# Block sums of the MLP's down weights formed in HBM by copies and accumulating transfers, ahead of the stages that use them

## The chip, the cores and the metric

The kernel runs on one core of one Trainium2 chip. The metric is the device time of one execution in microseconds (us). Shown for the kernel before are three timed runs and one profiled execution.

## The reference

A two-layer decoder trunk on 528 tokens (16 learned meta tokens and 512 inputs), model width 1024: layer 0 is a forgetting attention, layer 1 a gated linear recurrence (HGRN2), and each is followed by a gated MLP with a hidden width of 2816. The change concerns the last product of that MLP:

```python
def conv_ffn(h, norm_g, w_gate, w_up, conv_w, conv_b, w_down):
    xn = rms_norm(h, norm_g)
    a = xn @ w_gate
    ...
    return (jax.nn.silu(a) * (xn @ w_up)) @ w_down
```

`w_down` has 2816 x 1024 values in float32, once for each layer.

## The kernel before

Activations stand transposed: 128 features on the partitions, tokens along the free dimension. A matrix product is done in float32r, with each operand split in a high part and a low rest (`hi` and `lo`, a cast on ScalarE and a subtraction on VectorE), and three matmuls for a block: hi by hi, hi by rest, rest by hi. The stages stand one behind the other: attention (`fox`), MLP of layer 0 (`ffn`), recurrence (`hgrn`), MLP of layer 1 (`ffn` again). In the MLP the stretch of hidden features is worked off in two runs: a run of six (twelve blocks of 128 hidden features, in two halves of r = 6) and a run of five (ten blocks, r = 5).

In each run there are two parts:

- **The hidden part.** `hidden` makes one block of hidden features: two weight tiles `gu` (gate and up, 512 KB each, loaded by `weights`, line 191), 48 matmuls with each in layer 0 (24 of 512 columns with the up tile in layer 1), a causal convolution on VectorE (lines 1056 and 1057) and the gating. In layer 0 the two leading columns of the tile `A` are set to zero by GpSimd (line 1046), and the convolution reads them. `forms` then makes seven combinations of the token halves, as Strassen's scheme in Winograd's form needs them (the two index directions are the halves of the hidden features and the halves of the tokens).
- **The down part.** For each of four pairs of output blocks, `down` does seven products of r x 3 matmuls (126 in a run of six, 105 in a run of five), where four weight blocks w11, w12, w21, w22 (128 x 768 or 128 x 640 values) enter alone or as sums: s1 = w21 + w22, s2 = s1 + w11, s3 = s2 - w22 (that is w21 + w11), s4 = s2 + w12. Here the kernel before loads the four blocks and forms the four sums on VectorE at lines 1113, 1145, 1153 (by the helper at line 124) and 1156. All seven weight blocks are then split (`parts`: the cast at line 1097, the subtraction by line 124).

Buffers: `raw` has two (the `gu` weights, and w21 and w22 of a pair: w21's becomes s1 and then s2), `hi` and `lo` three each, `temp` eight of 768 columns (the tiles A, t, s, ta, tb of the hidden part, and w11, w12, s3, s4 of the down part). The four PSUM tiles of a pair are named psp (two), psc and psd.

What sets the order: each engine works off its instructions in the order that a scheduler has given them, which weighs the program by a simulated timeline. SP (SyncE) issues every transfer, in its own order, and an issue that waits holds back those behind it. GpSimd has only some memsets and, at the start, seven additions.

In the run of five of layer 0, VectorE and ScalarE also do the work for the next stage within the down part: squares and their sum (lines 268 and 269), and the split of finished rows of `h` (lines 275 and 276).

Of the kernel before, what the change touches and what calls it, by code (L numbers as in the profile page):

```python
# [12 lines left out]
F32 = mybir.dt.float32  # L13
# [4 lines left out]
ALU = mybir.AluOpType  # L18
# [3 lines left out]
P = 128  # L22
D = 1024
KT = D // P
# [2 lines left out]
HF = 16  # L27
NPAIR = 8
NEARLY = 4
FF = 2816  # L30
NF = FF // P
EPS = 1e-6
# [42 lines left out]
def halves(t0):  # L75

    n = (T - t0) // 4 * 2
    return [(t0, n), (t0 + n, T - t0 - n)]


class Builder:
# [44 lines left out]
    def setup(self):  # L126
        nc = self.nc
        cp = self.cp = self.pool("const")
        self.h = cp.tile([P, KT, T], F32, name="h")
        self.vec = cp.tile([P, V_END], F32, name="vec")  # L130
        nc.sync.dma_start(self.vec, self.a["vec"])
        self.wraw = self.pool("wraw", 2)
        self.whi = self.pool("whi", 3)
        self.wlo = self.pool("wlo", 3)
        q, k = (self.weights(self.a["wqk"][0, i], KT, parts=2) for i in range(2))
        order = [(q, 0), 0, (k, 0), 1, 2, 3, (q, 1), (k, 1), 4, 5, 6, 7]
        for x in order:
            if isinstance(x, int):
                nc.sync.dma_start(self.h[:, x, :], self.a["h0"][:, x, :])
            else:  # L140
                x[0][3][x[1]]()
        self.first = q[:3], k[:3]
        cst = cp.tile([P, C_END], F32, name="cst")
        self.cst = cst
        nc.sync.dma_start(cst, self.a["cst"])
        self.ident = cst[:, C_ID : C_ID + P]
        self.identr = cp.tile([P, P], F32R, name="identr")
        nc.vector.tensor_copy(self.identr, self.ident)
        self.xhi = cp.tile([P, KT, T], F32R, name="xhi")
        self.xlo = cp.tile([P, KT, T], F32R, name="xlo")  # L150
        self.x = [(self.xhi[:, k, :], self.xlo[:, k, :]) for k in range(KT)]
        self.rsb = cp.tile([P, T], F32, name="rsb")
        self.onesd = cp.tile([P, 2], F32, name="onesd")
        nc.vector.memset(self.onesd, 1.0 / D)
        self.tiny = self.pool("tiny", 2)
        self.sqp = self.pool("sqp", 2)
        self.ps = self.pool("ps", 1, PSUM)
        self.nbank = 0
        self.ss = None
# [16 lines left out]
    def weights(self, src, n, w=P, parts=1):  # L176

        nc = self.nc
        raw = self.wraw.tile([P, 8 * P], F32, name="raw", tag="raw")[:, : n * w]
        hi = self.whi.tile([P, 8 * P], F32R, name="hi", tag="hi")[:, : n * w]  # L180
        lo = self.wlo.tile([P, 8 * P], F32R, name="lo", tag="lo")[:, : n * w]

        def load(c):
            nc.sync.dma_start(raw[:, c], src[:, c])
            nc.scalar.copy(hi[:, c], raw[:, c])
            self.sub(lo[:, c], raw[:, c], hi[:, c].bitcast(F32))

        self.raw = raw
        u = hi.rearrange("p (k c) -> p k c", c=w), lo.rearrange("p (k c) -> p k c", c=w), n
        if parts == 1:  # L190
            nc.sync.dma_start(raw, src)
            nc.scalar.copy(hi, raw)  # L192
            self.sub(lo, raw, hi.bitcast(F32))
            return u
        m = n * w // parts
        return *u, [partial(load, slice(i * m, i * m + m)) for i in range(parts)]

    def proj_unit(self, ps, units, x, t0, tn, prev=None):

# [124 lines left out]
    def fox(self, ctx):  # L324
# [274 lines left out]
        def stage_p():  # L599

            for m in range(NEARLY):
                nc.sync.dma_start(self.h[:, m, :], a["h0"][:, m, :])
# [159 lines left out]
    def hgrn(self, ctx):  # L762
        nc, tc, a = self.nc, self.tc, self.a
        mm = nc.tensor.matmul
        full = [(0, 264), (264, 264)]
        late = halves(A1)
        sp = self.pool("hg1", 1, ctx=ctx)
        s2 = self.pool("hg2", 2, ctx=ctx)
        ohi = sp.tile([P, KT, T], F32R, name="ohi")
# [251 lines left out]
    def ffn(self, ctx, layer, a0, o0):  # L1021

        nc, a = self.nc, self.a
        ga, up = (halves(t0) if T - t0 > 512 else [(t0, T - t0)] for t0 in (a0, o0))
        gcol, cw, cb = ((V_FFN0, V_CW0, V_CB0), (V_FFN1, V_CW1, V_CB1))[layer]
        sp = self.pool(f"ffn1_{layer}", 1, ctx=ctx)
        s2 = self.pool(f"ffn2_{layer}", 2, ctx=ctx)
# [37 lines left out]
        def temp(w, name):  # L1065
            return s2.tile([P, 6 * P], F32, name=name, tag="temp", bufs=8)[:, :w]
# [25 lines left out]
        def parts(raw):  # L1092

            w = raw.shape[1]
            hi = self.whi.tile([P, 8 * P], F32R, name="hi", tag="hi")[:, :w]
            lo = self.wlo.tile([P, 8 * P], F32R, name="lo", tag="lo")[:, :w]
            nc.scalar.copy(hi, raw)  # L1097
            self.sub(lo, raw, hi.bitcast(F32))
            return hi, lo

        def block(mp, c0, r, m, half, raw):
            k0 = (c0 + half * r) * P
            nc.sync.dma_start(raw, a[f"dn{layer}"][2 * mp + m][:, k0 : k0 + r * P])
            return raw

        def ready(mp, c0, r):

            x, w22 = (self.wraw.tile([P, 8 * P], F32, name="raw", tag="raw")[:, : r * P] for _ in range(2))
            w11 = block(mp, c0, r, 0, 0, temp(r * P, "w11"))
            p11 = parts(w11)  # L1110
            block(mp, c0, r, 1, 0, x)
            block(mp, c0, r, 1, 1, w22)
            nc.vector.tensor_tensor(x, x, w22, ALU.add)
            return w11, x, w22, p11, parts(x)

        def down(mp, c0, r, fhi, flo, last, first):

            def product(ps, w, f, start):
                hi, lo = w
                mm = nc.tensor.matmul
                for k in range(r):
                    c = slice(k * P, k * P + P)
                    xh, xl = fhi[:, f, k, :], flo[:, f, k, :]
                    mm(ps, hi[:, c], xh, start=start and k == 0, stop=False, skip_group_check=not start)  # L1127
                    mm(ps, hi[:, c], xl, start=False, stop=False, skip_group_check=not start)  # L1128
                    mm(ps, lo[:, c], xh, start=False, stop=k == r - 1, skip_group_check=not start)  # L1129

            def put(m, half, ps, op, store=False):
                c = o0 + half * hw
                hv = self.h[:, 2 * mp + m, c : c + hw]
                nc.vector.tensor_tensor(hv, hv, ps, op)
                if store and last and layer == 1:
                    nc.sync.dma_start(a["out"][2 * mp + m][:, half * hw : half * hw + hw], hv)

            A, D = (self.bank("p")[:, :hw] for _ in range(2))
            B, C = (self.bank(x)[:, :hw] for x in "cd")
            w11, x, w22, p11, ps1 = first or ready(mp, c0, r)  # L1140
            product(A, p11, 0, True)
            nc.scalar.copy(B, A)
            product(D, ps1, 3, True)
            put(1, 1, D, ALU.subtract)
            nc.vector.tensor_tensor(x, x, w11, ALU.add)
            product(B, parts(x), 4, False)
            nc.scalar.copy(C, B)
            put(0, 1, B, ALU.add)
            w12 = block(mp, c0, r, 0, 1, temp(r * P, "w12"))
            product(A, parts(w12), 1, False)  # L1150
            put(0, 0, A, ALU.add, True)
            s3, s4 = temp(r * P, "s3"), temp(r * P, "s4")
            self.sub(s3, x, w22)
            product(C, parts(s3), 5, False)
            put(1, 1, C, ALU.subtract, True)
            nc.vector.tensor_tensor(s4, x, w12, ALU.add)
            product(D, parts(s4), 2, False)
            put(0, 1, D, ALU.add, True)
            product(C, parts(w22), 6, False)
            put(1, 0, C, ALU.subtract, True)  # L1160
            if last and layer == 0:
                self.sumsq(2 * mp)
                self.sumsq(2 * mp + 1)


        for x in "cd":
            nc.tensor.matmul(self.bank(x)[:, :hw], self.xhi[:, 0, :P], self.xhi[:, 0, :hw], start=True, stop=True)
        for c0, r in ((0, 6), (12, 5)):
            fhi, flo = (sp.tile([P, 7, 6, hw], F32R, name=nm, tag=nm)[:, :, :r, :] for nm in ("fhi", "flo"))
            first = []  # L1170
            for j in range(r):
                early = None if j < r - 1 else lambda: first.append(ready(0, c0, r))
                forms(j, c0, r, fhi, flo, early)
            for mp in range(KT // 2):
                down(mp, c0, r, fhi, flo, c0 > 0, first.pop() if first else None)
# [99 lines left out]
```

## Time and profile before

| What | Value |
|---|---|
| Median of three runs | 1494.14 us (1490.6 to 1495.14) |
| Profiled execution, its own time | 1491.77 us |
| Its span, first to last instruction | 1489.7 us |
| Mean granted TensorE clock | 0.994 |
| VectorE, ScalarE and GpSimd busy | 68%, 42%, 2% of the span |
| Transfers of the SP queue | 131.58 MB, 28.4% of the 16 DMA engines' span |
| Transfers issued by GpSimd | none |

The page gives busy time by engine, and groups of instructions by line of the kernel. The view of windows gives the busy time of each engine in a stretch, with the number of instructions that touch it, the granted clock (PEclk) and the share of DMA engines that were busy. PE is TensorE, PEld its weight loads, DVE VectorE, ACT ScalarE, POOL GpSimd, SP SyncE. The chain of waits is followed back from the last instruction, so it names only what the end hung on.

### The profile page before, as it was taken

The page shows a single profiled execution, that of the slowest core. Times are in us where ns is not written, and L with a number is a line of the kernel's source. Part 1 is how long each engine was busy: PE and PEld are TensorE (multiplying, and loading weights), DVE is VectorE, ACT ScalarE, POOL GpSimd, SP SyncE. Part 2 cuts the span into 40 slices and gives each one's busy share as a digit, 9 for nine tenths or more (in the row PEclk, how much of TensorE's full clock was granted, in tenths as well). Part 3 has the DMA queues.
Part 4 walks back from the last instruction along what each step waited for, and adds up shares of the span by engine and source line. Part 5 has one row for each costly group of instructions (what it writes and reads, how often), then busy time and mean ns, then how long its engine had stood idle before and what let it go on. Part 6 is the DMA issues. An engine that isn't in the chain of part 4 may idle for free.

```text
span 1489.7 us, 28745 instructions
## 1 busy us (share of the span) xinstructions
PE 1457.1 (98%) x11620; PEld 1361.3 (91%) x11620; DVE 1010.8 (68%) x2147; ACT 627.2 (42%) x1214; POOL 33.5 (2%) x113
## 2 busy tenths in 40 slices
PE   7999999999999999999989999999999999999998
PEld 6888888988999999999889999999999999999988
DVE  7555555776576787666876667677567667767676
ACT  5355555654343343333543333333343344343433
POOL 6000000000000000000000000000000000000000
PEclk9999999999999999999999999999999999999999
DMA  4433344412323222222221201211132223332232
GB/s 157 117 103 88 102 96 121 133 52 81 113 86 100 89 86 96 100 100 79 89 78 59 85 29 58 72 58 58 57 100 86 95 90 89 96 114 89 91 103 87
DMA packets 48283, 133.39 MB, mean 90 GB/s; under 512 B 7816, under 2 KB 10376, under 8 KB 48152
## 3 DMA queue, kind: packets, MB, share of 16 engines
q1 hardware_dynamic: 48152, 131.58, 28.4%
q8 instruction: 91, 1.49, 0.4%
q14 instruction: 40, 0.33, 0.1%
HBM read 116.10 MB, written 2.10 MB: 79 GB/s over the span
## 4 chain that ended last, share of the span: by engine, by line
PE 86%; DVE 7%; DMA 4%; ACT 2%; issue 1%; SPq 1%; ACTq 0%; DVEq 0%
PE psp L206 12%; PE psp L209 12%; PE psp L210 12%; PE pss L210 8%; PE pss L206 8%; PE pss L209 8%; PE psp L255 5%; DVE lo L124 2%; DMA raw<-dn 2%; PE psc L739 2%; PE pss L890 1%; PE psp L1127 1%; PE psp L1128 1%; PE psp L1129 1%; ACT hi L1097 1%
## 5 line engine op out<-in xcount | busy, mean ns | idle before, releaser
L206 PE MATMUL psp<-xhi,hi 128*128 128x264 f32 (+3 forms) x1160 | 353.2, 305 | 6.2 <-ACT xhi L275 6.2
L209 PE MATMUL psp<-xlo,hi 128*128 128x264 f32 (+3 forms) x1160 | 354.0, 305 | 3.5 <-DVE xlo L276 3.5
L210 PE MATMUL psp<-xhi,lo 128*128 128x264 f32 (+3 forms) x1160 | 353.1, 304 | 0.0
L192 ACT CAST hi<-raw 128x1024 fp32r<-128x1024 f32 (+1 forms) x170 | 174.8, 1030 | 345.5 <-PE psp L209 118.4
L124 DVE TENSOR_TENSOR lo<-raw,hi 128x1024 fp32r<-128x1024 f32 (+3 forms) x222 | 251.1, 1132 | 77.8 <-ACT hi L192 65.1
L206 PEld LDWEIGHTS psp<-xhi,hi 128*128 128x128 f32 x1160 | 219.7, 190 | 17.8 <-ACT xhi L275 6.2
L210 PE MATMUL pss<-xhi,lo 128*128 128x264 f32 (+2 forms) x824 | 233.7, 284 | 0.0
L209 PEld LDWEIGHTS psp<-xlo,hi 128*128 128x128 f32 x1160 | 220.0, 190 | 14.7 <-DVE xlo L276 4.2
L206 PE MATMUL pss<-xhi,hi 128*128 128x264 f32 (+2 forms) x824 | 233.1, 283 | 0.0
L209 PE MATMUL pss<-xlo,hi 128*128 128x264 f32 (+2 forms) x824 | 233.0, 283 | 0.0
L210 PEld LDWEIGHTS psp<-xhi,lo 128*128 128x128 f32 x1160 | 220.1, 190 | 8.8 <-issue 1.0
L206 PEld LDWEIGHTS pss<-xhi,hi 128*128 128x128 f32 x824 | 155.3, 189 | 0.9
L209 PEld LDWEIGHTS pss<-xlo,hi 128*128 128x128 f32 x824 | 155.1, 188 | 0.9
L210 PEld LDWEIGHTS pss<-xhi,lo 128*128 128x128 f32 x824 | 154.9, 188 | 0.0
L1127 PE MATMUL psp<-fhi,hi 128*128 128x264 f32 (+1 forms) x352 | 101.0, 287 | 2.8 <-ACT hi L1097 2.1
L1129 PE MATMUL psp<-fhi,lo 128*128 128x264 f32 (+1 forms) x352 | 100.5, 286 | 1.1 <-DVE lo L124 1.0
L1128 PE MATMUL psp<-flo,hi 128*128 128x264 f32 (+1 forms) x352 | 99.6, 283 | 0.0
L1127 PEld LDWEIGHTS psp<-fhi,hi 128*128 128x128 f32 x352 | 66.5, 189 | 4.8 <-ACT hi L1097 4.6
L255 PE MATMUL psp<-hi,xhi 128*128 128x256 f32 x232 | 67.4, 290 | 2.3 <-ACT v L542 2.3
L1129 PEld LDWEIGHTS psp<-fhi,lo 128*128 128x128 f32 x352 | 66.6, 189 | 2.5 <-DVE lo L124 2.5
L255 PE MATMUL psp<-lo,xhi 128*128 128x256 f32 x232 | 66.6, 287 | 0.2 <-DVE lo L124 0.2
L1128 PEld LDWEIGHTS psp<-flo,hi 128*128 128x128 f32 x352 | 66.5, 189 | 0.1
(434 smaller groups left out, 2966.0 us busy)
## 6 DMA issues: line engine op xcount, KB each, us to landing
raw<-gu SPq DMA_DIRECT2D x88, 512.0 KB
pk<-stg SPq DMA_DIRECT2D x48, 264.0 KB
raw<-wqk SPq DMA_DIRECT2D x14, 512.0 KB
raw<-dn SPq DMA_DIRECT2D x16, 384.0 KB
w<-dn SPq DMA_DIRECT2D x16, 384.0 KB
raw<-dn SPq DMA_DIRECT2D x16, 320.0 KB
w<-dn SPq DMA_DIRECT2D x16, 320.0 KB
raw<-wv SPq DMA_DIRECT2D x8, 512.0 KB
```

Of the source, the lines that this page charges most:

```text
L124: self.nc.vector.tensor_tensor(out, x, y, ALU.subtract)
L192: nc.scalar.copy(hi, raw)
L206: ins = mm(ps, hi[:, i, :], xh, start=k == 0, stop=False)
L209: mm(ps, hi[:, i, :], xl, start=False, stop=False)
L210: mm(ps, lo[:, i, :], xh, start=False, stop=k == total - 1)
L255: mm(ps[:tn, :256], y[:, t0 : t0 + tn], w, start=n == 0, stop=n == 23)
L739: ins = mm(o, v[:kn, j, 2 * (p % 2) + hd, :], w[hd][0], start=j == 0, stop=j == last)
L890: mm(pl[:, 64 * c : 64 * c + 64], kp[:, t0 : t0 + tn], q, start=True, stop=True)
L1097: nc.scalar.copy(hi, raw)
L1127: mm(ps, hi[:, c], xh, start=start and k == 0, stop=False, skip_group_check=not start)
L1128: mm(ps, hi[:, c], xl, start=False, stop=False, skip_group_check=not start)
L1129: mm(ps, lo[:, c], xh, start=False, stop=k == r - 1, skip_group_check=not start)
```

## The change

The four sums are no longer formed on VectorE. `sum_blocks` gives each its own tile in HBM: SP copies one block there (HBM to HBM), and GpSimd issues accumulating transfers that add the others (`out += y`, done by the DMA engines). For each pair and run that makes four copies and five accumulations (s2 takes two, and s4's reads the finished s2), over both layers 64 copies and 80 accumulations. One sum is put in after each weight load that `weights` does: those of layer 0 begin with the first `gu` tile of its MLP, those of layer 1 with the first weights of the recurrence. In the down part all seven blocks of a pair are loaded, three from `dn` and four from the sums, each into a buffer of `temp`, and are split as before. `block` and `ready` go, and the two `raw` buffers stay with the other weights.

```diff
+RUNS = [(0, 6), (12, 5)]
...
+        self.hbm = self.pool("hbm", 1, bass.MemoryType.DRAM)
+        self.sums = {}
+        self.summing = iter(())
...
         if parts == 1:
-            nc.sync.dma_start(raw, src)
+            self.load = nc.sync.dma_start(raw, src)
+            next(self.summing, None)
             nc.scalar.copy(hi, raw)
             self.sub(lo, raw, hi.bitcast(F32))
             return u
...
+    def sum_blocks(self, layer):
+
+        nc = self.nc
+        for mp, c0, r in [(mp, *run) for run in RUNS for mp in range(KT // 2)]:
+            src = lambda m, half: self.a[f"dn{layer}"][2 * mp + m][:, (c0 + half * r) * P : (c0 + half * r + r) * P]
+            s1, s2, s3, s4 = self.sums[layer, mp, c0] = [
+                self.hbm.tile([P, r * P], F32, name=f"s{i}", tag=f"s{i}_{layer}_{mp}_{c0}") for i in range(1, 5)
+            ]
+            w11, w12, w21, w22 = src(0, 0), src(0, 1), src(1, 0), src(1, 1)
+            for out, x, *rest in (s1, w21, w22), (s2, w21, w22, w11), (s3, w11, w21), (s4, w12, s2):
+                self.after(nc.sync.dma_start(out, x), self.load)
+                for y in rest:
+                    nc.gpsimd.dma_start(out, y, accum_op=ALU.add, max_dma_last_dim=4 * r * P)
+                yield 1
...
+        self.summing = self.sum_blocks(1)
...
+        if layer == 0:
+            self.summing = self.sum_blocks(0)
...
-        def ready(mp, c0, r):
-
-            x, w22 = (self.wraw.tile([P, 8 * P], F32, name="raw", tag="raw")[:, : r * P] for _ in range(2))
-            w11 = block(mp, c0, r, 0, 0, temp(r * P, "w11"))
-            p11 = parts(w11)
-            block(mp, c0, r, 1, 0, x)
-            block(mp, c0, r, 1, 1, w22)
-            nc.vector.tensor_tensor(x, x, w22, ALU.add)
-            return w11, x, w22, p11, parts(x)
+        def left(mp, c0, r, i):
+
+
+            raw = temp(r * P, "left")
+            if isinstance(i, int):
+                src = self.sums[layer, mp, c0][i - 1]
+            else:
+                k0 = (c0 + i[1] * r) * P
+                src = a[f"dn{layer}"][2 * mp + i[0]][:, k0 : k0 + r * P]
+            nc.sync.dma_start(raw, src)
+            return parts(raw)
...
-            w11, x, w22, p11, ps1 = first or ready(mp, c0, r)
-            product(A, p11, 0, True)
+            ws = lambda i: left(mp, c0, r, i)
+            product(A, first[0] if first else ws((0, 0)), 0, True)
             nc.scalar.copy(B, A)
-            product(D, ps1, 3, True)
+            product(D, first[1] if first else ws(1), 3, True)
             put(1, 1, D, ALU.subtract)
-            nc.vector.tensor_tensor(x, x, w11, ALU.add)
-            product(B, parts(x), 4, False)
+            product(B, ws(2), 4, False)
             nc.scalar.copy(C, B)
             put(0, 1, B, ALU.add)
-            w12 = block(mp, c0, r, 0, 1, temp(r * P, "w12"))
-            product(A, parts(w12), 1, False)
+            product(A, ws((0, 1)), 1, False)
             put(0, 0, A, ALU.add, True)
-            s3, s4 = temp(r * P, "s3"), temp(r * P, "s4")
-            self.sub(s3, x, w22)
-            product(C, parts(s3), 5, False)
+            product(C, ws(3), 5, False)
             put(1, 1, C, ALU.subtract, True)
-            nc.vector.tensor_tensor(s4, x, w12, ALU.add)
-            product(D, parts(s4), 2, False)
+            product(D, ws(4), 2, False)
             put(0, 1, D, ALU.add, True)
-            product(C, parts(w22), 6, False)
+            product(C, ws((1, 1)), 6, False)
             put(1, 0, C, ALU.subtract, True)
...
-                early = None if j < r - 1 else lambda: first.append(ready(0, c0, r))
+                early = None if j < r - 1 else lambda: first.append([left(0, c0, r, i) for i in ((0, 0), 1)])
```

The first place is GpSimd's queue, from the last memsets of the attention to the first of the recurrence, in the kernel before. `negm` and `ssum` belong to the attention, `rowsel`, `qp` and `qk` to the recurrence.

```order
L662 MEMSET ssum 128x6
L661 MEMSET negm 128x6
L1046 MEMSET A 128x2 x22
L774 MEMSET rowsel 128x512
L840 MEMSET qp 128x14
L844 MEMSET qk 128x21
```

In the changed kernel the same queue has accumulating transfers between those memsets. The piece is from the hidden part of the first run of layer 0: the `A` tiles are those of its third, fourth, fifth and sixth block of hidden features; s1 to s4 are the tiles in HBM.

```order
L1069 MEMSET A_5476 128x2
L215 DMA s1_5763<-dn0 128x768
L215 DMA s2_5764<-dn0 128x768
L1069 MEMSET A_5617 128x2
L215 DMA s2_5764<-dn0 128x768
L215 DMA s3_5765<-dn0 128x768
L1069 MEMSET A_5755 128x2
L215 DMA s4_5766<-s2_5764 128x768
L215 DMA s1_6042<-dn0 128x768
L1069 MEMSET A_5896 128x2
```

Each memset now stands behind two or three transfers; the second one into s2_5764 has to wait for the first, and that into s4_5766 for the second.

The second place is SP's queue at the end of the hidden part of that run, before: the last `gu` tile and the loads of the first two pairs.

```order
L191 DMA raw_6667<-gu0 128x1024
L1103 DMA raw_6673<-dn0 128x768
L1103 DMA raw_6674<-dn0 128x768
L1103 DMA w11_6675<-dn0 128x768
L1103 DMA w12_6873<-dn0 128x768
L1103 DMA w11_6977<-dn0 128x768
L1103 DMA w12_7053<-dn0 128x768
L1103 DMA raw_6975<-dn0 128x768
L1103 DMA raw_6976<-dn0 128x768
```

And in the changed kernel, where raw_7597 and raw_7609 are already `gu` tiles of the second run:

```order
L213 DMA s4_6603<-dn0 128x640
L195 DMA raw_7597<-gu0 128x1024
L213 DMA s1_7601<-dn0 128x640
L195 DMA raw_7609<-gu0 128x1024
L213 DMA s2_7602<-dn0 128x640
L1133 DMA left_6753<-dn0 128x768
L1133 DMA left_6759<-s1_5204 128x768
L1133 DMA left_6925<-s2_5205 128x768
L1133 DMA left_6951<-dn0 128x768
L1133 DMA left_6976<-s3_5206 128x768
L1133 DMA left_7001<-s4_5207 128x768
L1133 DMA left_7026<-dn0 128x768
```

A copy now follows every `gu` load, and the loads of a pair stand in the order of its products; each load of a sum waits for that sum's last accumulation.

The third place is VectorE at the second pair of layer 0's run of five, before; `raw_9011` is w21, then s1, then s2.

```order
L1113 TENSOR_TENSOR raw_9011<-raw_9011,raw_9012 128x640
L1134 TENSOR_TENSOR h_58<-h_58,psd_8861 128x264
L276 SCALAR_TENSOR_TENSOR xlo_101<-h_58,vec_59,xhi_100 128x528
L124 TENSOR_TENSOR lo_9023<-raw_9011,hi_9022 128x640
L269 TENSOR_TENSOR ss_9002<-ss_9002,sq_9004 128x528
L1145 TENSOR_TENSOR raw_9011<-raw_9011,w11_9013 128x640
L276 SCALAR_TENSOR_TENSOR xlo_101<-h_58,vec_59,xhi_100 128x528
L124 TENSOR_TENSOR s3_9102<-raw_9011,raw_9012 128x640
L1156 TENSOR_TENSOR s4_9103<-raw_9011,w12_9080 128x640
L1134 TENSOR_TENSOR h_58<-h_58,psp_9008 128x264
L124 TENSOR_TENSOR lo_9060<-raw_9011,hi_9059 128x640
```

The same place in the changed kernel:

```order
L125 TENSOR_TENSOR lo_9142<-left_9139,hi_9141 128x640
L1154 TENSOR_TENSOR h_58<-h_58,psd_8964 128x264
L296 SCALAR_TENSOR_TENSOR xlo_101<-h_58,vec_59,xhi_100 128x528
L125 TENSOR_TENSOR lo_9164<-left_9161,hi_9163 128x640
L289 TENSOR_TENSOR ss_9108<-ss_9108,sq_9110 128x528
L296 SCALAR_TENSOR_TENSOR xlo_101<-h_58,vec_59,xhi_100 128x528
L125 TENSOR_TENSOR lo_9187<-left_9184,hi_9186 128x640
L1154 TENSOR_TENSOR h_58<-h_58,psp_9114 128x264
```

The four sums are gone from it; the subtractions that give `lo`, the additions into `h` and the next stage's work stay in their order.

More of the change, by code (lines that the diff above doesn't have):

```diff
@@ L1099, in parts @@
             return hi, lo
[L1101 to L1104, printed above, removed]
-        def ready(mp, c0, r):
-            x, w22 = (self.wraw.tile([P, 8 * P], F32, name="raw", tag="raw")[:, : r * P] for _ in range(2))
-            w11 = block(mp, c0, r, 0, 0, temp(r * P, "w11"))
-            p11 = parts(w11)
-            block(mp, c0, r, 1, 0, x)
-            block(mp, c0, r, 1, 1, w22)
-            nc.vector.tensor_tensor(x, x, w22, ALU.add)
-            return w11, x, w22, p11, parts(x)
+        def left(mp, c0, r, i):
[7 more added lines that the diff above has]
+            return parts(raw)
         def down(mp, c0, r, fhi, flo, last, first):
@@ L1167, in ffn @@
             nc.tensor.matmul(self.bank(x)[:, :hw], self.xhi[:, 0, :P], self.xhi[:, 0, :hw], start=True, stop=True)
-        for c0, r in ((0, 6), (12, 5)):
+        for c0, r in RUNS:
             fhi, flo = (sp.tile([P, 7, 6, hw], F32R, name=nm, tag=nm)[:, :, :r, :] for nm in ("fhi", "flo"))
```

## The prediction, on record before the result

> **What bounds the kernel now.** I read the page first: which engine is busy, and how much idle time of it there is to win.
>
> ```profile
> span 1489.7 us, 28745 instructions
> ...
> PE 1457.1 (98%) x11620; PEld 1361.3 (91%) x11620; DVE 1010.8 (68%) x2147; ACT 627.2 (42%) x1214; POOL 33.5 (2%) x113
> ```
>
> TensorE is the bound; no more than 32.6 us are idle in all. Then the windows, cut from the first matmul of each of the four down runs to the first one behind it (layer 0: six, five; layer 1: six, five), with one hidden part and a calm stretch of layer 1 to compare.
>
> ```profile
> core 0: us, PE busy (x) PEld busy (x) DVE busy (x) ACT busy (x) POOL busy (x), PEclk, DMA share, GB/s
> 531.22:594.79 63.57, 62.40 (x506) 61.58 (x505) 49.65 (x73) 27.24 (x39) 0.20 (x2) 1.00 0.30 95
> 711.47:774.05 62.58, 56.08 (x422) 53.35 (x421) 50.81 (x83) 31.19 (x52) 0.00 (x0) 0.97 0.26 81
> 1254.50:1317.22 62.72, 61.01 (x505) 60.15 (x504) 49.97 (x73) 27.32 (x39) 0.00 (x0) 1.00 0.31 95
> 1430.44:1486.50 56.06, 52.75 (x421) 50.50 (x419) 43.15 (x70) 22.11 (x37) 0.00 (x0) 1.00 0.36 106
> 594.79:711.47 116.68, 116.68 (x963) 116.68 (x962) 80.17 (x132) 44.49 (x63) 0.80 (x8) 1.00 0.28 92
> ...
> 1276.00:1289.00 13.00, 13.00 (x112) 13.00 (x111) 9.63 (x14) 4.57 (x7) 0.00 (x0) 1.00 0.38 122
> ```
>
> Busy time flatters a matmul that waits, so I use the pace. The hidden part does ten blocks of 96 matmuls in 116.68 us: 0.1215 us each. The calm stretch of layer 1 holds 110 (two of its 112 lie over the edges): 0.118 each. At these paces the runs would take 504 x 0.1215 = 61.2, 420 x 0.1215 = 51.0, 504 x 0.118 = 59.5 and 420 x 0.118 = 49.6 us. They take 2.4, 11.6, 3.2 and 6.5 us more: **23.7 us** that the down runs lose, half of it in layer 0's run of five. There the granted clock is 0.97 as well, about 1.9 of the 11.6.
>
> What ends the waits in that run, from the view of waits (engine, tile and line, releaser: total us, times, longest):
>
> ```profile
> PE psc L1129 <- DVE lo L124: 2.5, 3, 1.3
> PE psc L1127 <- ACT hi L1097: 2.3, 3, 1.0
> PE psp L1127 <- ACT hi L1097: 0.7, 1, 0.7
> PE psp L1129 <- DVE lo L124: 0.6, 2, 0.4
> ```
>
> All are waits for a split weight block. The chain of waits says why it is late, here across the change of a pair (start, us, what):
>
> ```profile
> 736.10 0.84 DVE lo L124
> 736.95 2.93 DMA raw<-dn
> 739.97 0.82 DVE raw L1113
> ...
> 741.34 0.43 DVE h L1134
> ...
> 743.09 0.70 DVE ss L269
> 743.79 0.68 DVE xlo L276
> 744.47 0.74 DVE raw L1145
> 745.21 0.34 DVE h L1134
> 745.55 0.73 DVE s L124
> 746.28 0.74 DVE s L1156
> 747.02 0.74 DVE lo L124
> 747.81 0.39 PE psc L1129
> ```
>
> The last split of w22 frees a `raw` buffer, only then does the next pair's load start (2.93 us), s1 waits for it, and later three sums (L1145, L124, L1156) and a split stand in a row on VectorE while TensorE waits.
>
> **The change, part by part.** *Removed:* four sums for each of 16 pair-runs.
>
> ```profile
> L1113 DVE TENSOR_TENSOR raw<-raw 128x768 f32<-128x768 f32 (+1 forms) x16 | 14.3, 892 | 13.7 <-DMA raw<-dn 13.7
> L124 DVE TENSOR_TENSOR s<-raw 128x768 f32<-128x768 f32 (+1 forms) x16 | 14.2, 889 | 0.3
> L1145 DVE TENSOR_TENSOR raw<-raw,w 128x768 f32<-128x768 f32 (+1 forms) x16 | 14.2, 888 | 0.2
> L1156 DVE TENSOR_TENSOR s<-raw,w 128x768 f32<-128x768 f32 (+1 forms) x16 | 14.2, 886 | 0.0
> ```
>
> That is 56.9 us of VectorE, of which only the 23.7 us above can be on the path. *The load leaves the chain:* seven loads of a pair go round eight `temp` buffers, each free again after its split, so a load can be issued several products ahead instead of behind the split of w22. *What is late next:* of `hi` and `lo` there are three, so a block's cast waits for the end of the product three before it, and must be split two products later, in a run of five 2 x 15 x 0.1215 = 3.65 us.
>
> ```profile
> L124 DVE TENSOR_TENSOR lo<-raw,hi 128x640 fp32r<-128x640 f32 (+1 forms) x12 | 10.3, 855 | 1.1 <-ACT hi L192 0.5 <-ACT hi L1097 0.4
> L1097 ACT CAST hi<-raw 128x640 fp32r<-128x640 f32 x11 | 8.0, 728 | 9.6 <-DVE raw L1145 4.8 <-PE psp L1128 4.1 <-DVE raw L1113 0.6
> ```
>
> Cast 0.73 and split 0.86, and in VectorE's order at the change of a pair an addition into h (0.43), xlo (0.68) and ss (0.70): 3.4 us, only just covered. VectorE in all: 50.8 - 16 x 0.82 = 37.7 of 51.0 us. So I leave 3 to 4 of the 23.7 us standing (some half a microsecond a pair in layer 0's run of five, and the first pair of each run, which comes straight from the hidden part's tail on VectorE), and take a gain of **20 us**.
>
> *Added to the down runs:* three loads a pair. In the hidden part's window 0.28 of the engines' time moved 92 GB/s, so 329 GB/s when all are busy: 1.2 us for 384 KB, 1.0 for 320. Seven make 8.4 of 15.3 us and 7 of 12.8: beside the work, if the sums are there in time. If not, SP stops at a load of a sum and the loads queued behind it stop too; but layer 0's sums are begun with its first `gu` tiles, and layer 1's are spread over the whole recurrence:
>
> ```profile
> 850.00:1122.00 272.00, 272.00 (x2541) 256.14 (x2541) 183.69 (x480) 94.17 (x186) 0.92 (x8) 1.00 0.19 63
> ```
>
> *Added to the hidden part of layer 0* is the dear piece. Two blocks take 116.68 / 5 = 23.3 us and get four copies and five accumulations, the latter in GpSimd's queue in front of the memset of `A`, for which VectorE's convolution waits.
>
> ```profile
> 462.78 0.10 POOL L1046 MEMSET A<- 128x2 f32 x1 [14.90 <-DVE tb L124]
> ...
> 469.51 0.33 SPq L191 DMA_DIRECT2D raw<-gu  x1
> ...
> 479.92 1.23 DVE L124 TENSOR_TENSOR lo<-raw,hi 128x1024 fp32r<-128x1024 f32 x1 [0.57 <-ACT hi L192]
> 481.07 0.76 DVE L1056 SCALAR_TENSOR_TENSOR t<-A,vec,t 128x528 f32<-128x528 f32 x1
> ...
> L269 POOL TENSOR_TENSOR ss<-ss,sq 128x528 f32<-128x528 f32 x7 | 11.4, 1626 | 8.2 <-ACT sq L268 7.8
> ```
>
> Now the memset is done 18 us before its reader at 481.07. After, it stands behind an accumulation whose copy SP issues after the `gu` load of 469.51: two issues, some 1.6 us for the 512 KB ahead of it, 2.93 for the copy, then GpSimd's issue; done at about 476, 5 us to spare. The split at 479.92 is ready some 9 us before its use, so VectorE can be that much late before TensorE stands.
> In the trace there is no accumulation. Bounds for one, from issue to landing: 2.93 (the load, as it were one pass) and 8.8 us (read, read again, write: three such); below the load's time nothing can be, and a gain neither, since nobody needs it. I take two passes, 5.9, as two reads share the way in. Its issue: between SP's 0.33 and GpSimd's longest instruction, 1.63; I take 1.0. Two of the five wait for a predecessor, so four sums take 2 x 5.9 + 5 x 1.0 = 16.8 us (7.5 to 25.8), against 23.3. The forecast's cost is 0; at the upper end six such groups lag 15 us, all but 1 us inside the 14 us of slack.
> The Trainium skill (Collectives: The Full Stack, "The bandwidth ceiling") puts an adding transfer at half the rate of a copy, since it needs two source reads on one ring; by that the sum is the same 16.8. No run here shows it yet.
>
> **Sum.** Own time 1491.8 - 20 = 1471.8 us. The profiled run lies 2.4 us below the median of 1494.1; from that median, allowing 1 us for loads disturbed here and there, I forecast **1475 us**.
>
> **The rivals.**
> *A, another wait takes part of it* (0.18). The 3.4 of 3.65 us above has no reserve, and ScalarE's squares and xhi stand between the casts; or GpSimd lags by a few microseconds. Half of the 20 us stays: 1484. For it: two of the four waits above already end with a cast; against: VectorE loses a quarter of its work there.
> *B, nothing is won* (0.07). The loads of the sums come late, behind others on the same engines, and TensorE waits for DMA where it waited for splits: 1494.
> *C, slower: the DMA engines fill up in layer 0's hidden part* (0.16). Per 23.3 us they have 0.28 x 23.3 = 6.5 us of work, 4 x 1.2 = 4.8 of copies and five accumulations: at two passes 12, together 23.3, just full; at three 18, together 29.3. Then the group takes 29.3, GpSimd lags 6 us a group, six groups 36, less 14 of slack: 22 us lost against 20 won. So it decides at about 3.6 us of all engines for one accumulation. At 4.2 us the group is 32.3, the loss 40 and the time 1494 + 20 = 1514. For it: the sum of shares; against: a share counts waiting packets too, and later sums are of 320 KB.
> *D, slower: issues held up* (0.04). If each issue waited for the VectorE instruction under way, 1.2 us at 479.92, three passes and 1.63 us issues make 25.8 + 5 x 1.2 = 31.8: six groups lag 51, less 14 is 37, less 20: 1511. Against: these are all TENSOR_TENSOR and SCALAR_TENSOR_TENSOR.
> The Trainium skill (SBUF — State Buffer, "SBUF: two separate sides") warns of this: descriptors of a GpSimd transfer cannot be written while VectorE runs a 2-port-mode instruction. By the same page tensor_tensor has no such mode; nothing here shows it.
>
> **Numbers.** Forecast 0.53 (1469 to 1479), A 0.18, B 0.07, C 0.16, D 0.04, the rest 0.02 a gain of all 23.7 and more. What a measurement of this kernel can tell from no change is about 0.3%, 4.5 us, so faster is below 1489.6: 0.53 + 0.18 + 0.02 less a piece of A, 0.71; same 0.08; slower 0.21. The range from 1469 to 1503 leaves out the deeper gain and the greater part of C and D.
>
> **What would show it.** Right: down runs of about 61.5, 52.5, 60 and 51 us, no wait of TensorE for `lo` above half a microsecond, memsets of `A` some 5 us ahead of their convolution, hidden parts still at 116.7 us. A: casts or splits still end waits in the run of five. B: SP waits for accumulations. C: a DMA share near 1 from 400 to 530 us, and VectorE waiting for GpSimd's memsets, the first hidden part longer than 23.3 us for two blocks. D: the same waits with the DMA share low. The prediction is wrong if the hidden part of layer 0 grows by over 5 us, or the down runs keep over 8 of their 23.7 us.

## The result, and the profile after

The changed kernel took 1474.74 us (median of four runs, 1471.5 to 1480.18), the kernel before 1493.74 us in the same sitting (1490.6 to 1495.14): a ratio of 0.9879, 95% interval 0.9845 to 0.9913. The forecast was 1475. The profiled execution happens to be the longest of the four, 1480.18 us; so its trace shows more than the median does, and the excess is told below.

The page first:

```profile
span 1478.4 us, 29090 instructions
...
PE 1453.3 (98%) x11620; PEld 1362.2 (92%) x11620; DVE 963.9 (65%) x2083; ACT 627.4 (42%) x1214; POOL 99.0 (7%) x193
...
q1 hardware_dynamic: 64280, 171.95, 36.4%
q0 software_dynamic: 11520, 28.84, 12.3%
...
s<-dn POOLq DMA_DIRECT2D x32, 384.0 KB, 6.8
...
s<-dn POOLq DMA_DIRECT2D x32, 320.0 KB, 6.3
```

VectorE has lost 64 instructions and 47 us; a second queue, GpSimd's, has appeared with 80 accumulations that take 12.3% of all DMA engines' time. The windows of the changed kernel, cut as those of before: the four down runs, layer 0's second hidden part, most of its first one, and two pieces of the recurrence's opening.

```profile
core 0: us, PE busy (x) PEld busy (x) DVE busy (x) ACT busy (x) POOL busy (x), PEclk, DMA share, GB/s
532.32:594.91 62.59, 61.97 (x506) 61.54 (x505) 40.54 (x60) 27.47 (x40) 0.10 (x1) 1.00 0.52 164
711.58:763.76 52.18, 51.76 (x423) 51.30 (x421) 41.78 (x69) 32.03 (x53) 0.00 (x0) 1.00 0.52 154
1249.84:1310.82 60.98, 60.16 (x505) 59.92 (x504) 39.33 (x58) 27.30 (x39) 0.00 (x0) 1.00 0.50 157
1424.04:1475.16 51.12, 50.20 (x421) 49.91 (x419) 33.82 (x56) 22.32 (x37) 0.00 (x0) 1.00 0.62 188
594.91:711.58 116.67, 116.67 (x962) 116.67 (x961) 78.55 (x130) 44.67 (x63) 9.01 (x19) 1.00 0.54 153
408.00:525.00 117.00, 117.00 (x965) 117.00 (x964) 83.34 (x143) 46.24 (x67) 20.72 (x34) 1.00 0.93 232
784.00:791.04 7.04, 4.19 (x35) 4.01 (x35) 4.12 (x11) 2.33 (x3) 0.82 (x1) 0.96 0.97 231
791.04:797.50 6.46, 6.46 (x28) 5.65 (x29) 0.00 (x0) 0.10 (x1) 1.62 (x2) 0.52 0.86 210
```

The down runs sum to 226.87 us against 244.93 before: 18.1 of the 23.7 us are won, 10.4 of them in layer 0's run of five. (In two later executions of the changed kernel, again and pair below, they sum to 225.98 and 226.24, so 19.0 and 18.7 are won; the kernel before has one trace.) The hidden part is at its old pace (116.67 against 116.68), though the DMA engines are now 0.93 busy in the first one. What the views did not let me expect stands in the last two rows. TensorE's waits in the changed kernel, from the first down run on:

```profile
PE psd L258 <- DMA raw<-hv: 2.9, 1, 2.9
PE psc L1149 <- DVE lo L125: 2.5, 4, 0.9
```

The second row is what is left of the waits for splits, one for each run (0.3 to 0.9 us). The first is new: the `hv` weights of the recurrence come late. The chain of waits has that load:

```profile
782.48 8.43 DMA raw<-hv
```

It takes 8.43 us; SP has put the first copies of layer 1's sums beside the weight loads that open the recurrence, and the experiments below show that the wait comes from them. Behind the wait the granted clock is 0.52 for 6.5 us (28 matmuls at about twice their time). Both together make the stretch from the end of layer 0's MLP to layer 1's first down run 486.1 us (763.76 to 1249.84) against 480.5 before (774.05 to 1254.50): 5.6 us given back in this execution. So the profiled times are accounted for: 18.1 won, 5.6 given back, and 1.1 us by which the first down run begins later (532.32 against 531.22) make 11.4 of the 11.6 us between 1491.77 and 1480.18.

### The profile page after: what moved, and what is told of

Its sections match the earlier page's. It is cut to its first block, busy times and chain, and to the rows that moved or that the text cites. A ratio compares the mean times of both kernels' runs of the same rounds, so it can differ in the third digit from the quotient of the medians.

```text
span 1478.4 us, 29090 instructions
## 1 busy us (share of the span) xinstructions
PE 1453.3 (98%) x11620; PEld 1362.2 (92%) x11620; DVE 963.9 (65%) x2083; ACT 627.4 (42%) x1214; POOL 99.0 (7%) x193
## 3 DMA queue, kind: packets, MB, share of 16 engines
q1 hardware_dynamic: 64280, 171.95, 36.4%
q0 software_dynamic: 11520, 28.84, 12.3%
## 4 chain that ended last, share of the span: by engine, by line
PE 95%; DMA 2%; DVE 1%; ACT 1%; issue 1%; SPq 1%; DVEq 0%; ACTq 0%
PE psp L226 12%; PE psp L229 12%; PE psp L230 12%; PE pss L230 8%; PE pss L226 8%; PE pss L229 8%; PE psp L275 6%; PE psp L1149 3%; PE psp L1147 3%; PE psp L1148 3%; PE psc L759 2%; PE psd L1148 1%; PE psd L1149 1%; PE psd L1147 1%; PE pss L911 1%; PE pss L688 1%
## 5 line engine op out<-in xcount | busy, mean ns | idle before, releaser
L125 DVE TENSOR_TENSOR lo<-raw,hi 128x1024 fp32r<-128x1024 f32 (+1 forms) x174 | 208.3, 1199 | 66.8 <-ACT hi L197 62.9
L1120 ACT CAST hi<-left 128x768 fp32r<-128x768 f32 (+1 forms) x112 | 86.7, 780 | 114.5 <-PE psp L1148 42.1
L125 DVE TENSOR_TENSOR lo<-left,hi 128x768 fp32r<-128x768 f32 (+1 forms) x112 | 99.2, 891 | 49.3 <-ACT hi L1120 47.2
L215 POOL DMA_DIRECT2D s<-dn x64 | 52.7, 855 | 394.9 <-DMA s<-dn 337.2
L1074 DVE TENSOR_TENSOR A<-pss,rsb 128x258 f32<-128x258 f32 (+1 forms) x73 | 30.9, 426 | 55.2 <-PE pss L230 54.9
```

What stands on the lines that cost most here:

```text
L125: self.nc.vector.tensor_tensor(out, x, y, ALU.subtract)
L215: nc.gpsimd.dma_start(out, y, accum_op=ALU.add, max_dma_last_dim=4 * r * P)
L1074: nc.vector.tensor_tensor(A[:, 2 + t0 : 2 + t0 + tn], ps, self.rsb[:, t0 : t0 + tn], ALU.mult)
```

## The experiments

Theory at the start: the gain is the 18 us of the down runs; the sums cost nothing but the `hv` wait at the opening of the recurrence. Rivals: that wait was chance; the transfers disturb in many places; and, as to the gain, that it comes from VectorE's lighter row alone, or from the early loads alone.

**The change once more (again).** No edit.

> The changed kernel once more, as the partner of the others. Theory: the first sums of layer 1 stand among the weight loads that open the recurrence, and make TensorE wait for an hv load (2.9 us in the first profile, with 3 us of half clock behind it). Then this profile shows a wait of TensorE for DMA raw<-hv again, 2 to 4 us, and the time is 1472 to 1478. Rival: that wait was chance; no such wait here, same time.

1474.68 us (ratio 0.9881, 0.9862 to 0.9901). The wait was there again, but shorter than the 2 to 4 us that I expected:

```profile
PE psd L258 <- DMA raw<-hv: 0.8, 1, 0.8
```

No stretch at half clock followed it. The place is real, its length varies from one execution to the next.

**Later sums (later_sums).**

```diff
-        self.summing = self.sum_blocks(1)
+        self.summing = chain([0] * 8, self.sum_blocks(1))
```

> Layer 1's sums begin eight weight loads later, behind the opening of the recurrence. Theory (the hv wait comes from the sums beside it): no wait for hv, about 3 us less than the changed kernel, up to 6 where the half clock followed: 1469 to 1472. Rival (chance): same as the changed kernel within 1 us, about 1474.5.

1471.33 us (0.9865, 0.9845 to 0.9884). The wait for `hv` is gone from the view of waits. The windows say why; first the changed kernel's opening of the recurrence, then this one's:

```profile
767.00:790.00 23.00, 21.19 (x183) 19.93 (x175) 12.58 (x39) 8.96 (x14) 3.25 (x4) 1.00 0.92 259
```

```profile
767.00:790.00 23.00, 23.00 (x190) 22.45 (x190) 12.61 (x30) 8.21 (x13) 0.00 (x0) 1.00 0.28 93
```

The DMA share falls from 0.92 to 0.28 and TensorE works through. In this run SP also issues the `hv` load 4.8 us earlier (at 777.68 us, against 782.48), so it alone does not tell the missing sums from the earlier load. The next run does: it forms no sums, SP issues that load at 782.09, the DMA share from 767 to 790 us is 0.39, and TensorE has no wait for `hv`. That the first sums cause the wait is shown by the two together; that the median is 3.3 us lower points the same way, but the two intervals overlap.

**The down part alone (plain_blocks).** `sum_blocks` is not run, and where a sum was loaded a plain block is (so the output is another one).

```diff
-            if isinstance(i, int):
-                src = self.sums[layer, mp, c0][i - 1]
-            else:
-                k0 = (c0 + i[1] * r) * P
-                src = a[f"dn{layer}"][2 * mp + i[0]][:, k0 : k0 + r * P]
+            if isinstance(i, int):
+                i = ((1, 0), (0, 0), (1, 0), (0, 1))[i - 1]
+            k0 = (c0 + i[1] * r) * P
+            src = a[f"dn{layer}"][2 * mp + i[0]][:, k0 : k0 + r * P]
```

> No sums are formed; where the change loads a sum this loads a plain block of the same size, so the output is another one. It is the down part alone. Theory: the whole gain lies in the down runs (18 us in the traces) and forming costs nothing but the hv wait: 1470 to 1472, down runs of 62.6, 52.2, 61.0 and 51.1 us as in the changed kernel. Rival (the sums' transfers disturb loads in many places): over 5 us below the changed kernel, under 1469, and down runs shorter by a microsecond or more each.

1473.55 us (0.9873, 0.9854 to 0.9892), above the 1470 to 1472 of my theory and 1.1 us under its partner (again), with overlapping intervals; its down runs sum to 225.73 us where the partner's had 225.98. So the accumulations take next to nothing from the down runs; the rival of disturbed loads is out.

**The sums formed for nobody (formed_only).** The kernel before with `sum_blocks` of the change added; the down part is the old one.

```diff
-            nc.sync.dma_start(raw, src)
+            self.load = nc.sync.dma_start(raw, src)
+            next(self.summing, None)
```

> The sums are formed in HBM as in the change, but nobody reads them; the down part is that of the kernel before, with its sums on VectorE. Theory: 1494 to 1498, layer 0's hidden parts at 116.7 us as before, the only loss at the opening of the recurrence. Rival (DMA engines fill up): over 1500, with the loss in layer 0's hidden parts or in the down loads.

1497.34 us, 4.7 above its partner of 1492.64 (1.0033, 1.0019 to 1.0047). The waits and the second hidden part of layer 0:

```profile
PE psd L258 <- DMA raw<-hv: 3.5, 1, 3.5
```

```profile
710.54:775.85 65.31, 59.02 (x422) 56.40 (x421) 51.01 (x83) 31.35 (x53) 0.81 (x1) 0.92 0.29 85
...
593.87:710.54 116.67, 116.67 (x963) 116.67 (x961) 79.95 (x132) 45.83 (x64) 8.21 (x18) 1.00 0.46 135
```

The hidden part again pays nothing. Most of the price stands at the opening: from the end of layer 0's MLP to layer 1's first down run it is 485.4 us (775.85 to 1261.29) against 480.5. Beside it, the run of five is 2.7 us longer than before: its granted clock of 0.92 comes from three lowered places (0.80 from 727 to 735 us, 0.86 from 743 to 751, 0.74 from 764 to 768) where the kernel before has one. Why there are more of them is open.

**The sums stay, the loads come early (vsum_temp).** The kernel before; only w21 and w22 go to `temp`.

```diff
-            x, w22 = (self.wraw.tile([P, 8 * P], F32, name="raw", tag="raw")[:, : r * P] for _ in range(2))
+            x, w22 = (temp(r * P, nm) for nm in ("w21", "w22"))
```

> The kernel before, its four sums still on VectorE, but with w21 and w22 in the ring of eight temp buffers in place of the two raw buffers, so that a pair's loads are issued before the last split of the pair ahead. Theory (the late load at the change of a pair and the row of sums on VectorE share the 23.7 us): about half of the change's gain, 1480 to 1486, most of it outside layer 0's run of five. Rival 1 (the row of sums alone): 1490 to 1493. Rival 2 (the late load alone): 1474 to 1477.

1477.93 us (0.9896, 0.9882 to 0.9911): 15.6 us under the 1493.5 of its partner, more than my theory gave it and just short of rival 2 (the late load alone). Its down runs:

```profile
534.05:597.66 63.61, 62.38 (x506) 61.59 (x505) 50.55 (x73) 27.41 (x39) 0.20 (x2) 1.00 0.28 83
714.33:767.88 53.55, 52.27 (x422) 51.31 (x421) 50.48 (x84) 32.10 (x54) 0.00 (x0) 1.00 0.26 77
1247.97:1309.80 61.83, 60.59 (x506) 59.97 (x504) 50.65 (x73) 27.96 (x40) 0.00 (x0) 1.00 0.29 85
1423.01:1473.96 50.95, 50.36 (x421) 49.91 (x419) 42.62 (x70) 22.53 (x37) 0.00 (x0) 1.00 0.37 120
```

They sum to 229.94 us. With all its sums, VectorE is 50.48 us busy in layer 0's run of five, and the run takes 53.55 instead of 62.58: 9.0 of the gain lie in the run where my theory had the least of it. Two loads put into another ring of buffers bring 15.0 of the 18.1 us, with no sum in HBM.

**VectorE's work back, on the loaded block (adds_back).** The changed kernel; the maximum of a block with itself leaves it as it is.

```diff
-            return parts(raw)
+            return parts(raw if isinstance(i, tuple) else nc.vector.tensor_tensor(raw, raw, raw, ALU.max) and raw)
```

> The changed kernel with one VectorE instruction of the old size (the maximum of the block with itself, which leaves it as it is) ahead of the split of each loaded sum: VectorE has its 56.9 us again, with the loads of the change. Theory: layer 0's run of five, where VectorE had 50.8 us of work for 51, grows by 3 to 6 us, the other three runs by at most 1 each: 1478 to 1483. Rival 1 (the row of sums alone): down runs near those of before, 1490 or more. Rival 2 (the late load alone): 1474 to 1476.

1492.76 us (0.9995, 0.9986 to 1.0004): the whole gain is gone, and my range of 1478 to 1483 was wrong. VectorE's waits in layer 1's run of five, and TensorE's:

```profile
DVE left L1134 <- DMA left<-s: 7.2, 7, 1.8
```

```profile
PE psd L1147 <- DVE h L1154: 2.7, 2, 1.4
PE psc L1147 <- ACT hi L1120: 1.4, 1, 1.4
```

The added instruction waits for its own load, and behind it in VectorE's order wait the additions into `h` that free TensorE's PSUM tile. ScalarE's cast, too, now has to wait for the added instruction. In the changed kernel VectorE needs a loaded block only after ScalarE's cast of it. So this run does not price VectorE's time alone; it prices a VectorE instruction that waits for a transfer. How the lost 18 us divide is not shown.

**The partner of the next runs (pair).** The changed kernel a third time; free_work, two_raw and best ran beside it.

> The changed kernel as the partner of the next three: 1473 to 1476. As to the hv load at the opening of the recurrence: a wait of TensorE between 0 and 3 us, and a stretch at half clock behind it only where the wait is near 3 us.

1472.75 us (0.9881, 0.9863 to 0.99), a little under the range, with a wait for `hv` of 0.7 us and full clock behind it.

**VectorE's work back, waiting for nothing (free_work).** Therefore four instructions of the same size for each pair that read a finished tile, tied behind an addition into `h`.

```diff
+        def extra(fhi, r):
+            out = self.wraw.tile([P, 8 * P], F32, name="extra", tag="raw")[:, : r * P]
+            x = fhi[:, 0, :, :].bitcast(F32).rearrange("p k t -> p (k t)")[:, : r * P]
+            self.after(nc.vector.tensor_tensor(out, x, x, ALU.max), self.put)
```

> The changed kernel with four VectorE instructions of the old size for each pair (the maximum of a part of fhi with itself, into an idle raw buffer), tied behind the additions into h, whose inputs are all there: VectorE's 56.9 us are back, and no load or wait with them. Theory (the late load was the cost, the sums' own time on VectorE is nearly covered): 1475 to 1480, the growth in layer 0's run of five. Rival (VectorE's time was the cost; the run with the maximum on the loaded block lost its gain by it): 1488 or more.

1487.12 us (0.996, 0.9947 to 0.9972), above the range of my theory and just short of the rival's. The sums over the four down runs, of its partner and of this run:

```profile
sum 226.24, PE 223.81 PEld 222.61 DVE 154.98 ACT 108.98 POOL 0.10; mean PE 55.95 PEld 55.65 DVE 38.74 ACT 27.25 POOL 0.03
```

```profile
sum 234.17, PE 225.89 PEld 224.07 DVE 195.22 ACT 106.56 POOL 1.28; mean PE 56.47 PEld 56.02 DVE 48.80 ACT 26.64 POOL 0.32
```

7.9 us of the 14.0 between the two spans (1484.8 and 1470.8) are in the down runs. One wait in layer 1's run of six is the largest piece:

```profile
PE psc L1155 <- DVE lo L125: 2.6, 1, 2.6
```

It is the third product of the first pair, ahead of whose split two added instructions stand in a row. A lowered clock follows it (0.57 from 1257.2 to 1261.2 us), and the run is 3.2 us longer than its partner's; so is layer 0's run of five. The other 6 us lie outside the down runs, 4.8 of them in the stretch up to layer 1's first down run. The tile that I gave the extra instructions is one of the two `raw` buffers, which the weight loads use. SP's view of waits has 50.9 us in six waits of weight loads for an added instruction, but in the partner weight loads wait 42.1 us in three for additions into `h`; so whether the added instructions hold these loads up, and whether the 6 us come from that, stays open.

**Every load behind a split (two_raw).** The changed kernel, seven loads of a pair in two buffers, no sums on VectorE.

```diff
-            raw = temp(r * P, "left")
+            raw = self.wraw.tile([P, 8 * P], F32, name="left", tag="raw")[:, : r * P]
```

> The changed kernel with its seven loads of a pair in the two raw buffers in place of the eight of temp: no sums on VectorE, but every load behind a split. Theory (late loads are the cost): for each block 0.33 us of issue, 2.9 of load, 0.75 of cast and 0.85 of split go round two buffers, 2.4 us a block against products of 2.2 and 1.8: down runs longer by 6 us (six) and 9 (five), 1495 to 1510. Rival (VectorE's sums were the cost): 1475 to 1480.

1523.37 us (1.02, 1.0182 to 1.0218), slower than the kernel before and above my range. TensorE waits for a split 42 times (38 of them in the rows of `lo` here), although VectorE has a quarter less work in the down runs than before:

```profile
PE psp L1149 <- DVE lo L125: 10.2, 27, 0.5
...
PE psp L1147 <- ACT hi L1120: 5.0, 7, 1.3
PE psd L1149 <- DVE lo L125: 3.6, 11, 0.5
```

```profile
531.25:600.82 69.57, 65.77 (x506) 62.43 (x505) 36.27 (x57) 26.48 (x38) 0.42 (x1) 1.00 0.52 153
717.89:782.26 64.37, 57.95 (x423) 52.56 (x421) 41.23 (x70) 32.05 (x52) 0.39 (x1) 1.00 0.49 144
```

69.57 and 64.37 us over 28 blocks are 2.48 and 2.30 us a block; 2.4 was expected from issue, load, cast and split round two buffers. The four runs sum to 267.41 us, 40.5 above the changed kernel's: loads behind a split alone can cost more than all that the change won.

**Twice the sums (twice).** A second set of sums into tiles that nobody reads.

```diff
+                twin = self.hbm.tile([P, r * P], F32, name="twin", tag=f"twin{layer}_{k}")
+                for o in out, twin:
```

> Each sum is formed twice, the second time into a tile that nobody reads: twice the copies and accumulations. The rival of the prediction in which the DMA engines fill up in layer 0's hidden part gives for two blocks 6.5 us of loads, 9.6 of copies and ten accumulations of about 2.3 us of all engines (as the first profile of the change has them), 39 us against 23.3: 15 us behind a group, some 80 us after six groups, so 1540 to 1570 with a DMA share near 1. If instead the waits of GpSimd for landings decide: under 1500, with memsets of A late by a few microseconds. If nothing decides: 1475 to 1480.

1524.96 us (1.0211, 1.0193 to 1.023), 50 us above the change. Layer 0's first hidden part, from where it falls behind to its end, and ScalarE's longest waits there:

```profile
445.00:554.00 109.00, 95.94 (x697) 92.40 (x696) 62.61 (x108) 35.09 (x50) 29.47 (x43) 0.92 1.07 283
```

```profile
ACT hi L197 <- DMA raw<-gu: 31.0, 10, 4.8
```

The DMA engines are full (a share over 1 is overlapping packets), and the `gu` loads come late. 697 matmuls are 7.3 blocks: 30 us for two, against 23.3. This is the prediction's rival C, at its place and with full engines, but by another path: C had VectorE waiting for GpSimd's memsets, and from 440 to 561 us VectorE has no such wait; what comes late are the `gu` loads themselves. The 39 us that I expected for two blocks, and with them 1540 us or more, were too dear. By this run's page an accumulation took 1.95 us of all engines (20.5% of 1519.4 us, over 160 of them), and some of the sums there have 320 KB in place of 384; that makes about 35 us, and the rest of the difference is open. Behind the hidden part the first down run takes 72.26 us against 62.59.

**The third block early as well (later_three, best).** On top of the later sums, the third block of a run's first pair is loaded and split with the first two.

```diff
-                early = None if j < r - 1 else lambda: first.append([left(0, c0, r, i) for i in ((0, 0), 1)])
+                early = None if j < r - 1 else lambda: first.append([left(0, c0, r, i) for i in ((0, 0), 1, 2)])
...
-            product(B, ws(2), 4, False)
+            product(B, first[2] if first else ws(2), 4, False)
```

> Layer 1's sums begin eight loads later, and the third block of each run's first pair is loaded and split with the first two, ahead of the last forms. Theory (what is left of the waits stands at the third product of each run): the waits of TensorE for lo in the down runs (2.0 us) go, 1468 to 1470 together with the later sums. Rival (the split only moves ahead of the forms, and other products wait for those): the same as with the later sums alone, 1471 to 1473, or worse.

1470.83 us (0.9841, 0.9826 to 0.9857), just above my range and not clear of the 1471.33 of the later sums alone. Beside the partner of above (pair) it ran once more:

> Later sums and three early blocks once more, beside its partner. Theory: the 2 us of waits for lo and the hv wait of 1 to 3 us are gone: 3 to 5 us below the partner, the intervals of the ratios apart. Rival (the waits come back as others): within 2 us of the partner.

1469.04 us (0.9838, 0.9825 to 0.9851) against 1472.75 (0.9881, 0.9863 to 0.99): the intervals are apart, and it beats both kernels. It holds both edits; how they divide the 3.7 us is not shown.

```profile
531.59:593.04 61.45, 61.45 (x506) 61.45 (x505) 39.89 (x60) 27.61 (x39) 0.10 (x1) 1.00 0.51 163
709.71:760.84 51.13, 51.13 (x422) 51.13 (x421) 41.65 (x69) 32.15 (x53) 0.00 (x0) 1.00 0.49 149
1241.63:1301.44 59.81, 59.81 (x506) 59.80 (x504) 39.36 (x58) 27.40 (x39) 0.00 (x0) 1.00 0.52 159
1414.65:1464.50 49.85, 49.85 (x421) 49.79 (x419) 33.62 (x56) 22.49 (x37) 0.00 (x0) 1.00 0.61 192
```

TensorE is busy for the whole of each down run, and the four sum to 222.24 us, against the 221.3 that the prediction worked out from the paces.

## Why the prediction was right, step by step

- **What the down runs lose, and what comes back.** 23.7 us lost, 20 forecast as gain, 18.1 measured. 3 to 4 us were to stay; 5.6 did (4.7 and 4.9 in again and pair). Where they stay was half right. No half microsecond a pair is left in layer 0's run of five, where one wait of 0.3 us for a split remains: the 3.4 us of VectorE's work against 3.65 was cover enough, and rival A had no place. That holds although VectorE was 41.78 us busy there, not the 37.7 of the forecast. The first pair is what is left: the profiled runs lie 1.2 to 1.5 us above their paces, 0.3 to 0.9 us of it the wait of the third product for its split, longer than the half microsecond that the prediction allowed in two of the runs. The early split of that block takes the waits away, and the runs sum to 222.24 us where the partner's sum to 226.24 (best, pair).
- **Which part of the edit brings it.** The prediction named two, the load that leaves the chain and the four sums that leave VectorE, and did not divide the gain. The first alone brings 15.0 of the 18.1 us (vsum_temp). For the second 3.1 us are left by that run, while VectorE's time put back into the changed kernel costs 7.9 us in the down runs (free_work). The two do not add up: what a VectorE instruction costs hangs on what stands behind it in the order and whether it has to wait. That both lie below the load's share of the down runs is shown; the exact division is not, and neither is the source of the 6 us that free_work loses outside them.
- **The accumulation.** Issue 1.0 us was taken, the row of 64 says 0.855; 5.9 us to landing, measured 6.8 and 6.3 (medians). Time of all engines: 12.3% of 1478.4 us over 80 is 2.27 us each, 2.4 taken (two passes of 1.2). By the two queue rows the accumulating queue moved 28.84 MB in 181.8 us, 159 GB/s, and SP's 171.95 MB in 538 us, 320 GB/s: half. The Trainium skill (Collectives: The Full Stack, "The bandwidth ceiling") gives the adding transfer half the copy's rate; here the trace agrees.
- **The hidden part at no cost.** Right in the time, 116.67 us, but with less to spare than was said. I had the memset of `A` 5 us ahead of its convolution; at the same block it now ends 0.6 us ahead:

```profile
481.13 0.40 POOL L1069 MEMSET A<- 128x2 f32 x1
...
482.16 0.76 DVE L1079 SCALAR_TENSOR_TENSOR t<-A,vec,t 128x528 f32<-128x528 f32 x1
```

From 420 us on the margin lies between 0.6 and 9.3 us. Once before that, VectorE did wait for it; TensorE works through (117.00 of 117.00 us above), so VectorE's slack, which the prediction counted on, covered the wait:

```profile
DVE t L1079 <- POOL A L1069: 2.3, 1, 2.3
```

- **Rival C.** Its sum for the change was "just full", its point 3.6 us an accumulation; measured 0.93 full and 2.27. Doubling the transfers fills the engines and slows the hidden part, through late `gu` loads (twice). **Rival D** is out: GpSimd's issues do not grow beside VectorE's work. The 64 of this row take 0.809 to 1.130 us, half of them 0.812 or less.

```profile
L215 POOL DMA_DIRECT2D s<-dn x64 | 52.7, 855 | 394.9 <-DMA s<-dn 337.2 <-PE psp L275 20.8 <-PE pss L890 20.4
```

- **The step that failed: layer 1's sums at no cost.** They were covered by a window of the recurrence that begins at 850 us, where the DMA share was 0.19. But SP begins them at the recurrence's first loads, some 85 us earlier, where it issues six weight loads and six copies within 21 us (767.36 to 788.02). Measured: a DMA share of 0.92 there, a wait of 0.7 to 2.9 us for `hv`, and at its longest a stretch at half clock behind it. The 1 us that the forecast allowed "for loads disturbed here and there" is about what it cost in the median (1.1 us between again and plain_blocks, whose intervals overlap), but 5.6 us in the profiled execution. That the median came out within half a microsecond is luck in part: the down runs brought 18.1 to 19.0 us in three traces, not 20, and the kernel before had a median of 1493.74 us in that sitting, not the 1494.14 that the forecast began from.

## What to carry to other kernels

When a sum before a matmul looks dear, first ask whether its load could have been issued earlier: here two loads in another ring of buffers brought five sixths of what leaving the sums out brought. What an instruction on an in-order engine costs hangs on whether its data is there: 40 us of added VectorE work with its data at hand cost 7.9 us of the down runs, and instructions of the same size that wait for a load cost the whole gain, with what stands behind them waiting too. A share of DMA averaged over a stage hides its opening: cut the window where the new transfers begin, and let them begin after the stage's own first loads.

## What the runs showed of the hardware

- A wait of TensorE of 2.9 us was followed by 6.5 us at a granted clock of 0.52 (the windows above), one of 0.8 us in the same place was not. In free_work a wait of 2.6 us was followed by 4 us at 0.57. In the kernel before, the run of five has a stretch like it with no single wait over 1.3 us ahead:

```profile
760.00:764.00 4.00, 2.29 (x14) 1.65 (x13) 4.00 (x7) 1.98 (x3) 0.00 (x0) 1.00 0.00 0
764.00:768.00 4.00, 4.00 (x22) 4.00 (x22) 1.95 (x4) 1.00 (x2) 0.00 (x0) 0.57 0.38 131
```

The Trainium skill (TensorE: Matmul & The Clock Gate, "HAM oscillation — how this bites in real kernels") has idle gaps over about 3.4 us lower the clock. The measurements decide here: gaps of 2.9 and 2.6 us had a lowered clock behind them, and so had 4 us that were 57% busy.
- An accumulating transfer from HBM to HBM took 2.27 us of all 16 engines for 320 to 384 KB in the changed kernel (1.95 in twice), about twice what SP's queue took for as many bytes (159 GB/s against 320). It landed in 5.4 to 6.8 us (medians by size and source), and in 8.1 to 11.0 where the sums were doubled.
